# Turning the delta rule's values and outputs, and two attention heads' rows, in 32x32 blocks on VectorE, with the blocks put in their places by the DMA that stores or loads the tile

## The chip, the cores and the metric

The kernel runs on one core of one Trainium2 chip. The metric is the device time of one execution in microseconds (us). Before the change three executions took 1235.09, 1235.05 and 1234.37 us, so the median is 1235.05 us.

## The reference: what is computed

One decoder layer on x of 1024 tokens by 1024 features, all float32. A first RMS norm feeds one input projection `proj = h @ w_in`, whose columns go to two groups that mix the tokens:

- differential attention, 4 heads with two 64-wide softmax maps and 128-wide values: `(softmax(q1 k1^T) - lam * softmax(q2 k2^T)) v`, then an RMS norm per head;
- a gated delta rule, 4 heads, key and value width 128. q, k and v pass a causal convolution of width 4 and SiLU, q and k are normalised, and a state is carried over chunks of tokens:

```
v_new = u - w @ state
o     = (q * exp(g)) @ state + qk @ v_new
state = state * exp(g_last) + k_dec^T @ v_new
```

The output o is normalised per head and multiplied by `silu(z)`.

```
x = x + concat(da_o, dn_o) @ w_out
x = x + square(relu(rms_norm(x) @ w_up)) @ w_down
```

## The kernel before the change, in words

A matmul contracts over the partition axis, so an operand has to lie with the contracted feature on the 128 partitions. Where a tile lies with tokens on the partitions it is turned first. Before the change every such turn is a transpose on TensorE (PE) against an identity matrix: it lands in a PSUM bank, from which VectorE (DVE) or ScalarE (ACT) takes it. The big products keep float32 accuracy by splitting each operand into a rounded part and a rest (`hH`/`hL`, `wH`/`wL`) and doing three fp32r matmuls.

The kernel runs in these stages, with line numbers of the profile:

1. Norm, z and gates (lines 306 to 645).
2. The delta rule's projection, `dn_proj` (666), for k, then q, then v. Each call gives one head h and one half hf of the tokens, 512 tokens, with features on the partitions. For v the loop of lines 851 to 857 turns the four 128x128 tiles on PE (`transposed`, 713, recorded at line 716), scales them by the column `vsc` with one DVE operation (854) and writes them with `park` (701), one DMA of 256 KB, to slot 2 of `park_d` in DRAM. `horner` (797) inverts the chunk matrices for two heads at a time with short dependent matmuls (810, 818), between the v tiles. Its blocks are loaded by 32 small DMAs (804).
3. From line 880 on the order of PE's instructions is written by a planner, `Interleave` (39 to 105). Streams of work yield the time from which they may go on and the PSUM bank they need. The planner keeps a clock of its own with estimated costs, and `flow.hold` says until when a bank is taken. The planner fixes the order for PE alone. The orders on DVE, ACT, GpSimd (POOL) and SyncE (SP) are made by a scheduler when the kernel is built. Every engine then takes its instructions strictly in order. The streams, in order of priority:
   - `scan` (902): the state recurrence over 8 chunks c. `load(c)` (907) brings four 192 KB pieces, one per head, from `park_d` into one of two `pka` buffers (910). Four matmuls (918) feed a DVE operation on slot 2 of `pka` (922), and four more (930), a copy (932), four more (941) and the new state (947) follow.
   - `scan_out` (956): the chunk's output. Matmuls (970, 977), a sum of squares (984), a reciprocal root, four DVE products with the gate (989) and a DMA on POOL's queue (991) that writes the 128x512 tile `oc` to `mixn_d`.
   - `da_turns` (1020): turns the attention's q and k (1028, 1029) in one of the two `px` PSUM banks and stores them from POOL's queue (1034).
   - `mix_loads` (1287) and `mixed` (1298): loads each tile `mt` of `mixn_d` (1295) and each tile of attention rows, and turns all four 128-column blocks on PE (`turn`, 1278, through `to_hT`, 293, transposes at 298) in a `px` bank, then ACT and DVE write `hH` and `hL` (303, 304). A tile's place in `hH` is free only when the last input projection unit is done with that tile.
   - `values` (1222): for each head and block of queries the transposes of the probabilities (1238), the product with the values (1250) in a `px` bank, an ACT copy (1259) and square (1260), a reciprocal root, and a DVE product (1264). Heads 0 and 1 write their rows to `mixa_d` (1266); for heads 2 and 3 the tile `rows_of[tb]` is loaded with the two first heads' rows (1231) and filled up.
   - `scores` (1141), `da_units` (1041, the input projection for the attention, lines 1067 to 1069) and `outproj` (1325, the output projection, lines 1340 to 1342).

   The reciprocal roots (`rstd`, 288) go through POOL's power operation (291): named `rn` for the attention's q and k norm, `of` for the outputs.
4. The MLP, products at lines 1515 to 1517 and 1813 to 1815, which ends the kernel.

`add` registers a stream with its priority, and the planner's loop takes the first stream that may go on:

```python
    flow.add(0, scan(), SCAN_START)
    flow.add(2, values())
    flow.add(3, scores())
    flow.add(1.6, da_turns())
    flow.add(4, da_units())
    flow.add(1.4, mix_loads())
    flow.add(1.5, mixed())
    flow.add(5, outproj())
```

The functions that the diff touches, as they were:

Of the kernel before, what the change touches and what calls it, by code (L numbers as in the profile page):

```python
# [9 lines left out]
F32 = mybir.dt.float32  # L10
# [110 lines left out]
def tile_hymba_layer(  # L121
# [579 lines left out]
    def park(h, hf, slot, src):  # L701
        nc.sync.dma_start(park_d[h, 4 * hf:4 * hf + 4, :, slot, :].rearrange("c p d -> p c d"), v4(src))

    def cols4(t, h, hf):
        return t[:, 8 * h + 4 * hf:8 * h + 4 * hf + 4]

# [142 lines left out]

    heads = [((h, h + 1), hf) for hf in range(2) for h in (0, 2)]  # L850
    for h, hf, v2 in skew(dn_proj(2)):
        ps = transposed(v2)
        vs = ta("kn", 2)
        V.tensor_tensor(v4(vs), v4(ps), bc_col(cols4(vsc, h, hf)), ALU.mult)
        park(h, hf, 2, vs)
        if hf == 0:
            horner(*heads.pop(0))

# [43 lines left out]
    def scan():  # L902
        St = {}
        psA = pA.tile([P, 512], F32, name="ps_A")
        PA = {h: psA[:, h * P:(h + 1) * P] for h in range(HEADS)}

        def load(c):
            pka = sb.tile([P, HEADS, 3, P], F32, tag="pka", name="pka", bufs=2)
            for h in range(HEADS):
                nc.sync.dma_start(pka[:, h], park_d[h, c, :, 0:3, :])  # L910
            return pka

        nxt = load(0)
        for c in range(NT):
            pk, rr_, yy = nxt, {}, {}
            if c > 0:
                for h in range(HEADS):
                    T.matmul(PA[h], pk[:, h, 0, :], St[h], start=True, stop=True)
                for h in range(HEADS):
                    i = cidx(h, c)  # L920
                    rr_[h] = sb.tile([P, P], F32, tag="sr", name="sr", bufs=4)
                    V.scalar_tensor_tensor(rr_[h], PA[h], neg_eg[:, i:i + 1], pk[:, h, 2, :], ALU.mult, ALU.add)
                flow.pe(4 * MM)
                yield flow.chain(*[vec(P, 60)] * 4), None
            else:
                for h in range(HEADS):
                    rr_[h] = pk[:, h, 2, :]
            for h in range(HEADS):
                Wc = W[h, c // 4][:, (c % 4) * P:(c % 4 + 1) * P]
                T.matmul(PA[h], Wc, rr_[h], start=True, stop=True)  # L930
            y4 = sb.tile([P, 512], F32, tag="sy", name="sy", bufs=2)
            S.copy(y4, psA)
            if c + 1 < NT:
                nxt = load(c + 1)
            flow.pe(4 * MM)
            yield flow.chain(act(512)), None
            Sold = dict(St)
            for h in range(HEADS):
                yy[h] = y4[:, h * P:(h + 1) * P]
                if c < NT - 1:  # L940
                    T.matmul(PA[h], pk[:, h, 1, :], yy[h], start=True, stop=True)
            if c < NT - 1:
                for h in range(HEADS):
                    i = cidx(h, c)
                    Sn = sb.tile([P, P], F32, tag=f"S{h}", name=f"S{h}", bufs=2)
                    if c > 0:
                        V.scalar_tensor_tensor(Sn, St[h], elast[:, i:i + 1], PA[h], ALU.mult, ALU.add)
                    else:
                        V.tensor_copy(Sn, PA[h])
                    St[h] = Sn  # L950
                flow.pe(4 * MM)
            flow.add(1, scan_out(c, Sold, yy), 0, "pB")
            if c < NT - 1:
                yield flow.chain(*[vec(P, 60)] * 4), None

    def scan_out(c, Sold, yy):
        pkb = {}
        for h in range(HEADS):
            pkb[h] = sb.tile([P, 2, P], F32, tag="pkb", name="pkb", bufs=5)
            nc.sync.dma_start(pkb[h], park_d[h, c, :, 3:5, :])  # L960
        zgt = sb.tile([P, 512], F32, tag="zgt", name="zgt", bufs=1)
        nc.sync.dma_start(zgt, zg_d[c])
        oc = sb.tile([P, 512], F32, tag="oc", name="oc", bufs=2)
        so = sb.tile([P, 4], F32, tag="so", name="so", bufs=2)
        osq = sb.tile([P, P], F32, tag="osq", name="osq", bufs=1)
        yield flow.now + 2500, "pB"
        if c > 0:
            o1 = pB.tile([P, 512], F32, tag="pB", name="ps_o1")
            for h in range(HEADS):
                T.matmul(o1[:, h * P:(h + 1) * P], pkb[h][:, 0, :], Sold[h], start=True, stop=True)  # L970
            V.tensor_tensor(v4(oc), v4(o1), bc_col(eg[:, c::8]), ALU.mult)
            flow.pe(4 * MM)
            flow.hold("pB", flow.chain(vec(512)))
            yield flow.now, "pB"
        o2 = pB.tile([P, 512], F32, tag="pB", name="ps_o2")
        for h in range(HEADS):
            T.matmul(o2[:, h * P:(h + 1) * P], pkb[h][:, 1, :], yy[h], start=True, stop=True)
        if c > 0:
# [16 lines left out]
        flow.chain(*[act(P, True)] * 4, vec(4), powr(4), vec(4), *[vec(P, 60)] * 4, start=t)  # L995
# [226 lines left out]
    def values():  # L1222
        for _ in order:
# [3 lines left out]
            if h == 2:  # L1227
                while "ax" not in pools or len(rows_of) + len([x for x in loads if not x[3]]) > 1:
                    yield flow.now + 50, None
                rows_of[tb] = pools["ax"].tile([P, 512], F32, tag="mx", name="mx", bufs=2)  # L1230
                nc.sync.dma_start(rows_of[tb][:, 0:256], mixa_d[tb])
            ats = []
            for g in range(0, tb + 1, 4):
                r = yield from flow.bank("px")
# [29 lines left out]
            V.scalar_tensor_tensor(om, om, f, dawb, ALU.mult, ALU.mult)  # L1264
            if h < 2:
                nc.gpsimd.dma_start(mixa_d[tb, :, h * P:(h + 1) * P], om)
            flow.pe((tb + 1) * MM)
            t = flow.chain(act(P))
            flow.hold(r, t)
            t = flow.chain(act(P, True), vec(1), powr(1), vec(1), vec(P, 60), start=t)  # L1270
# [5 lines left out]
    landed, hns = {}, {}  # L1276

    def turn(r, src, t, tb, k0, keep=None):
        to_hT(src, tb, lambda: bank_tile(px, r, "ps_tr"), k0, 4, keep)
# [7 lines left out]
    def mix_loads():  # L1287
        while not (pre and state["scan"]):
            yield flow.now + 200, None
        for i, t in enumerate(tiles):  # L1290
            while i >= 2 + state["mixed"]:
                yield flow.now + 50, None
            mt = pools["a2"].tile([P, 512], F32, tag="mt", name="mt", bufs=2)
            with tc.issue_after(newest["SP"].ins):
                nc.sync.dma_start(mt, mixn_d[t])
            loads.append((mt, flow.now + MIX_T, t, 4))

    def mixed():
        for i in range(2 * NT):

            while not any(x[1] <= flow.now and x[2] in over for x in loads):
                yield flow.now + 50, None
            x = min((x for x in loads if x[2] in over), key=lambda x: x[1])
            r = yield from flow.bank("px")
            loads.remove(x)
            turn(r, *x)
            state["mixed"] += x[3] == 4
        while not state["attn"]:
            yield flow.now + 50, None
        scctx.close()  # L1310
# [607 lines left out]
```

## Time and profile before

| | |
|---|---|
| median of three executions | 1235.05 us |
| the profiled execution | 1234.74 us |
| its span, first to last instruction | 1233.0 us |
| PE busy | 1217.3 us, 99% of the span |
| DVE busy | 824.7 us, 67% |
| ACT busy | 624.2 us, 51% |
| POOL busy | 151.3 us, 12% |
| bytes moved by DMA | 202.12 MB, mean 164 GB/s |
| granted TensorE clock | 1.000 |

The profile shows one execution. It has a page with shares and groups of instructions, and its trace can be asked for the instructions of a line or of a tile, for a stretch of time, for waits, and for the chain of work that ended last. PE's records overlap: a matmul's record lasts from its start to its last result, while the next one starts long before, so the busy share says that PE is never without a record, not how fast it goes. The step from one start to the next is the cost of a matmul.

### The profile page before, as it was taken

The numbers are of one execution on the slowest core, as the hardware profiler recorded it, in microseconds if no ns is written. First come the engines' busy times: TensorE is split into PE (matmuls) and PEld (weight loads), VectorE is DVE, ScalarE is ACT, GpSimd is POOL, SyncE is SP. The second block draws the span as 40 slices with busy tenths as digits, with TensorE's granted clock in tenths as the row PEclk, the third lists the DMA queues.
The fourth block names the chain that finished last, engine by engine and source line by source line (L and its number), as shares of the span: only waits on it lengthen the run. The fifth ranks groups of instructions, "written<-read, shape, count | busy, mean of one in ns | idle before, by whom it ended". The sixth has DMA issues, their size and how long they took to land.

```text
span 1233.0 us, 18819 instructions
## 1 busy us (share of the span) xinstructions
PE 1217.3 (99%) x6823; PEld 1054.3 (86%) x6823; DVE 824.7 (67%) x1524; ACT 624.2 (51%) x1249; POOL 151.3 (12%) x215
## 2 busy tenths in 40 slices
PE   9999999999999999999999999999999999999998
PEld 8978888898999998888888888888888888888886
DVE  6868796556647657777799544565569755777543
ACT  6588553344346555566666544444564333333330
POOL 2411110043434421001200000000000000000000
PEclk9999999999999999999999999999999999999999
DMA  9344653278748756323437434444479645423301
GB/s 350 98 115 122 163 162 104 63 234 240 231 148 252 232 162 159 85 77 108 157 117 255 172 122 151 171 170 153 155 241 382 234 179 184 163 103 103 137 35 69
DMA packets 143301, 202.12 MB, mean 164 GB/s; under 512 B 20920, under 2 KB 98280, under 8 KB 143208
## 3 DMA queue, kind: packets, MB, share of 16 engines
q1 hardware_dynamic: 138584, 187.28, 46.9%
q0 software_dynamic: 4480, 13.64, 2.9%
q8 instruction: 54, 0.88, 0.3%
q14 instruction: 39, 0.32, 0.1%
q10 hardware_dynamic: 144, 0.00, 0.0%
HBM read 135.86 MB, written 65.01 MB: 163 GB/s over the span
## 4 chain that ended last, share of the span: by engine, by line
PE 88%; DVE 4%; DMA 3%; ACT 2%; issue 2%; POOL 1%; SPq 1%; POOLq 0%; DVEq 0%; ACTq 0%
PE X L1517 4%; PE X L1515 4%; PE X L1516 4%; PE X L1814 4%; PE X L1815 4%; PE X L1813 4%; PE ps_dn L265 3%; PE ps_dn L267 3%; PE ps_dn L266 3%; PE ps_qk L1067 3%; PE ps_qk L1068 3%; PE ps_qk L1069 3%; PE ps_o L1250 2%; PE Y L1515 2%; PE Y L1517 2%; PE Y L1516 2%
## 5 line engine op out<-in xcount | busy, mean ns | idle before, releaser
L1433 ACT CAST hH<-ur 128x1024 fp32r<-128x1024 f32 x56 | 58.9, 1051 | 173.4 <-PE Y L1814 89.8
L1434 DVE TENSOR_TENSOR hL<-ur,hH 128x1024 fp32r<-128x1024 f32 x56 | 68.3, 1223 | 79.4 <-ACT hH L1433 79.4
L1067 PE MATMUL ps_qk<-wH,hH 128*128 128x256 f32 x384 | 114.3, 298 | 0.0
L1069 PE MATMUL ps_qk<-wH,hL 128*128 128x256 f32 x384 | 108.7, 283 | 0.0
L1068 PE MATMUL ps_qk<-wL,hH 128*128 128x256 f32 x384 | 108.4, 282 | 0.0
L1434 DVE TENSOR_TENSOR op<-raw,op 128x1024 fp32r<-128x1024 f32 x48 | 58.7, 1223 | 74.2 <-PE X L1516 41.1
L1813 PE MATMUL X<-hH 128*128 128x512 f32 x224 | 87.1, 389 | 0.0
L1814 PE MATMUL X<-hL,hH 128*128 128x512 f32 x224 | 87.1, 389 | 0.0
L1815 PE MATMUL X<-hH,hL 128*128 128x512 f32 x224 | 87.1, 389 | 0.0
L265 PE MATMUL ps_dn<-hH,wH 128*128 128x512 f32 x192 | 76.3, 397 | 0.2 <-ACT cp L678 0.2
L267 PE MATMUL ps_dn<-hH,wL 128*128 128x512 f32 x192 | 75.8, 396 | 0.0
L266 PE MATMUL ps_dn<-hL,wH 128*128 128x512 f32 x192 | 75.8, 395 | 0.0
L1068 PEld LDWEIGHTS ps_qk<-wL,hH 128*128 128x128 f32 x384 | 73.4, 191 | 0.2
L1067 PEld LDWEIGHTS ps_qk<-wH,hH 128*128 128x128 f32 x384 | 73.3, 191 | 0.2
L1069 PEld LDWEIGHTS ps_qk<-wH,hL 128*128 128x128 f32 x384 | 73.1, 190 | 0.0
L1434 DVE TENSOR_TENSOR hL<-dw,hH 128x1024 fp32r<-128x1024 f32 x56 | 68.2, 1218 | 0.9 <-ACT hH L1433 0.9
L1433 ACT CAST op<-raw 128x1024 fp32r<-128x1024 f32 x48 | 50.4, 1052 | 35.7 <-PE Y L1517 19.9
L1433 ACT CAST hH<-dw 128x1024 fp32r<-128x1024 f32 x56 | 58.7, 1048 | 10.7 <-DMA dw<-in_w_down_dram 5.0
L1205 ACT ACTIVATE pexp<-pexp,mx 128x128 f32<-128x128 f32 (+7 forms) x64 | 49.7, 777 | 25.1 <-DVE mx L1204 24.5
L682 DVE SCALAR_TENSOR_TENSOR cy<-cp,pv,cy 128x512 f32<-128x512 f32 x72 | 53.7, 747 | 8.1 <-ACT cy L680 7.3
L1340 PE MATMUL ps_op<-wH,hH 128*128 128x512 f32 x128 | 53.0, 414 | 0.0
L1515 PE MATMUL Y<-hH,op 128*128 128x512 f32 x128 | 49.9, 390 | 0.4 <-DVE ua L1555 0.4
(370 smaller groups left out, 3429.1 us busy)
## 6 DMA issues: line engine op xcount, KB each, us to landing
ur<-ud SPq DMA_DIRECT2D x28, 1024.0 KB, 5.0
raw<-in_w_up_dram SPq DMA_DIRECT2D x32, 512.0 KB, 3.9
dw<-in_w_down_dram SPq DMA_DIRECT2D x32, 512.0 KB, 6.8
wraw<-in_w_units_dram SPq DMA_DIRECT2D x48, 256.0 KB, 3.7
qk_d<-qa POOLq DMA_DIRECT2D x32, 256.0 KB, 4.3
ud<-ua SPq DMA_DIRECT2D x16, 512.0 KB, 4.2
ud<-s SPq DMA_DIRECT2D x16, 512.0 KB, 2.7
pka<-park_d SPq DMA_DIRECT2D x32, 192.0 KB, 4.8
```

What stands on the lines that cost most here:

```text
L265: T.matmul(ps, lh(k), rh(k), start=(k == 0), stop=False)
L266: T.matmul(ps, lh(k), rl(k), start=False, stop=False)
L267: T.matmul(ps, ll(k), rh(k), start=False, stop=(k == n - 1))
L1067: T.matmul(ps[:, :256], hH[:, k, sl], wh[:, k, :], start=(k == 0), stop=False)
L1068: T.matmul(ps[:, :256], hH[:, k, sl], wl[:, k, :], start=False, stop=False)
L1069: T.matmul(ps[:, :256], hL[:, k, sl], wh[:, k, :], start=False, stop=(k == KB - 1))
L1433: S.copy(dst[0], src)
L1434: V.tensor_tensor(dst[1], src, dst[0].bitcast(F32), ALU.subtract)
L1515: T.matmul(ps, op[0][:, k, cs], h[0][:, k, :], start=start and k == 0, stop=False, skip_group_check=True)
L1813: T.matmul(bank[t], v[0][:, j, sl], v[2][:, j], start=s0, stop=False, skip_group_check=True)
L1814: T.matmul(bank[t], v[0][:, j, sl], v[3][:, j], start=False, stop=False, skip_group_check=True)
L1815: T.matmul(bank[t], v[1][:, j, sl], v[2][:, j], start=False, stop=s1, skip_group_check=True)
```

## The change

VectorE has an operation that transposes each 32x32 block of a tile in its own place. To make a 128x128 transpose of it, block (a, b) has still to go to place (b, a). The change does the first half on DVE and lets a DMA do the second.

- v tiles: the four PE transposes and the DVE scaling go. DVE block-transposes the 128x512 tile, and four DMAs (`put_blocks`) write it to `park_d` in pieces of 32 elements. The scaling by `vsc` moves into the scan: `scale(c, pk)` on POOL, one product on the 128x4x128 slot 2 of each `pka` buffer, after its load.
- scan outputs: the four products write into `zgt` instead of `oc`, DVE block-transposes `zgt` into `oc`, and the store to `mixn_d` is unchanged. `mix_loads` reads each tile with four DMAs (`get_blocks`). The tile then lies with features on the partitions, and `mixed` only writes `hH` and `hL` from it (`settle`), with no PE transpose and no `px` bank.
- heads 0 and 1: the DVE product writes to PSUM, into the third quarter of the bank that held the result, a DVE block transpose brings it to `om`, and the bank is planned as held until then. The rows are read with `get_blocks`, and `turn_last` turns only the two blocks of heads 2 and 3 on PE.

```diff
+    def put_blocks(dst, src):
+        for a in range(4):
+            s = slice(32 * a, 32 * a + 32)
+            nc.sync.dma_start(dst[:, s].rearrange("(b s) r -> s b r", s=32),
+                              src[s].rearrange("s (b r) -> s b r", r=32))
+
+    def get_blocks(dst, src):
+        k = dst.shape[1] // P
+        src = src.rearrange("(a s) (k b r) -> b s k a r", s=32, k=k, r=32)
+        for b in range(4):
+            nc.sync.dma_start(dst[32 * b:32 * b + 32].rearrange("s (k a r) -> s k a r", k=k, r=32), src[b])
...
     for h, hf, v2 in skew(dn_proj(2)):
-        ps = transposed(v2)
         vs = ta("kn", 2)
-        V.tensor_tensor(v4(vs), v4(ps), bc_col(cols4(vsc, h, hf)), ALU.mult)
-        park(h, hf, 2, vs)
+        V.transpose(vs, v2)
+        put_blocks(park_d[h, 4 * hf:4 * hf + 4, :, 2, :].rearrange("c p d -> (c p) d"), vs)
...
+        def scale(c, pk):
+            G.tensor_tensor(pk[:, :, 2, :], pk[:, :, 2, :], bc_col(vsc[:, c::8]), ALU.mult)
+
         nxt = load(0)
+        scale(0, nxt)
...
             flow.add(1, scan_out(c, Sold, yy), 0, "pB")
+            if c + 1 < NT:
+                scale(c + 1, nxt)
...
-            V.scalar_tensor_tensor(oc[:, h * P:(h + 1) * P], oc[:, h * P:(h + 1) * P], f[:, h:h + 1],
-                                   zgt[:, h * P:(h + 1) * P], ALU.mult, ALU.mult)
+            hs = slice(h * P, (h + 1) * P)
+            V.scalar_tensor_tensor(zgt[:, hs], oc[:, hs], f[:, h:h + 1], zgt[:, hs], ALU.mult, ALU.mult)
+        V.transpose(oc, zgt)
         nc.gpsimd.dma_start(mixn_d[c], oc)
...
-                nc.sync.dma_start(rows_of[tb][:, 0:256], mixa_d[tb])
+                get_blocks(rows_of[tb][:, 0:256], mixa_d[tb])
...
+            if h < 2:
+                V.scalar_tensor_tensor(po[:, 2 * P:3 * P], om, f, dawb, ALU.mult, ALU.mult)
+                V.transpose(om, po[:, 2 * P:3 * P])
+                nc.gpsimd.dma_start(mixa_d[tb, :, h * P:(h + 1) * P], om)
+                flow.hold(r, flow.chain(act(P, True), vec(1), powr(1), vec(1), vec(P, 60), vec(P, 60), start=t))
+                continue
...
+    def settle(src, tb, ks, t=None):
+        sl = slice(tb * P, (tb + 1) * P)
+        sv = src.rearrange("p (k t) -> p k t", t=P)
+        S.copy(hH[:, ks, sl], sv)
+        V.tensor_tensor(hL[:, ks, sl], sv, hH[:, ks, sl].bitcast(F32), ALU.subtract)
...
+    def turn_last(r, src, t, tb):
+        settle(src[:, 0:256], tb, slice(0, 2))
+        ps = bank_tile(px, r, "ps_tr")
+        for j in (2, 3):
+            T.transpose(ps[:, j * P:(j + 1) * P], src[:, j * P:(j + 1) * P], ident)
...
-                nc.sync.dma_start(mt, mixn_d[t])
+                get_blocks(mt, mixn_d[t])
...
+            if x[3] == 4:
+                loads.remove(x)
+                landed[x[2], 4] = settle(x[0], x[2], slice(4, 8))
+                state["mixed"] += 1
+                continue
             r = yield from flow.bank("px")
             loads.remove(x)
-            turn(r, *x)
-            state["mixed"] += x[3] == 4
+            turn_last(r, *x[:3])
```

More of the change, by code (lines that the diff above doesn't have):

```diff
@@ L994, in scan_out @@
         flow.hold("pB", t)
-        flow.chain(*[act(P, True)] * 4, vec(4), powr(4), vec(4), *[vec(P, 60)] * 4, start=t)
+        flow.chain(*[act(P, True)] * 4, vec(4), powr(4), vec(4), *[vec(P, 60)] * 4, vec(512, 100), start=t)
         if c == NT - 1:
@@ L1263, in values @@
             V.tensor_tensor(f, f, ri[:, 0:1], ALU.mult)
-            V.scalar_tensor_tensor(om, om, f, dawb, ALU.mult, ALU.mult)
-            if h < 2:
-                nc.gpsimd.dma_start(mixa_d[tb, :, h * P:(h + 1) * P], om)
             flow.pe((tb + 1) * MM)
             t = flow.chain(act(P))
+            if h < 2:
[4 more added lines that the diff above has]
+                continue
+            V.scalar_tensor_tensor(om, om, f, dawb, ALU.mult, ALU.mult)
+            t = flow.chain(act(P, True), start=t)
             flow.hold(r, t)
-            t = flow.chain(act(P, True), vec(1), powr(1), vec(1), vec(P, 60), start=t)
+            t = flow.chain(vec(1), powr(1), vec(1), vec(P, 60), start=t)
             if h == 3:
@@ L1276, in tile_hymba_layer @@
     landed, hns = {}, {}
+    def settle(src, tb, ks, t=None):
[3 more added lines that the diff above has]
+        V.tensor_tensor(hL[:, ks, sl], sv, hH[:, ks, sl].bitcast(F32), ALU.subtract)
+        n = P * (ks.stop - ks.start)
+        return flow.chain(act(n), vec(n), start=t)
+    def turn_last(r, src, t, tb):
[3 more added lines that the diff above has]
+            T.transpose(ps[:, j * P:(j + 1) * P], src[:, j * P:(j + 1) * P], ident)
+        flow.pe(2 * TR)
+        t = settle(ps[:, 256:512], tb, slice(2, 4))
+        flow.hold(r, t)
+        landed[tb, 0] = t
     def turn(r, src, t, tb, k0, keep=None):
```

## The prediction, made before the changed kernel ran

> **What bounds the kernel now.** I read the page's shares first, then its slices, then the shares of the chain that ended last.
>
> ```profile
> span 1233.0 us, 18819 instructions
> PE 1217.3 (99%) x6823; PEld 1054.3 (86%) x6823; DVE 824.7 (67%) x1524; ACT 624.2 (51%) x1249; POOL 151.3 (12%) x215
> PE   9999999999999999999999999999999999999998
> PE 88%; DVE 4%; DMA 3%; ACT 2%; issue 2%; POOL 1%; SPq 1%; POOLq 0%; DVEq 0%; ACTq 0%
> ```
>
> PE is busy in every slice and carries 88% of the chain. Next, the view by stage: columns are the stretch and its length, busy us of PE, of its weight loads, of DVE, ACT and POOL, then clock, DMA share and GB/s.
>
> ```profile
> 185.00:256.00 71.00, 70.40 (x538) 61.98 (x537) 42.83 (x85) 24.75 (x59) 3.82 (x5) 1.00 0.33 95
> 256.00:350.00 94.00, 90.69 (x774) 89.81 (x773) 58.14 (x177) 41.63 (x126) 37.55 (x48) 1.00 0.74 231
> 350.00:460.00 110.00, 108.35 (x881) 105.97 (x881) 68.06 (x207) 65.80 (x182) 46.13 (x67) 1.00 0.70 206
> 460.00:585.00 125.00, 123.89 (x737) 108.28 (x736) 92.06 (x248) 77.25 (x203) 15.15 (x28) 1.00 0.38 107
> 640.00:1233.00 593.00, 588.14 (x2593) 486.49 (x2592) 374.70 (x344) 258.59 (x261) 0.00 (x0) 1.00 0.47 167
> ```
>
> The v tiles fall in 185 to 256, the scan in 256 to 350, the turned scan outputs from 430 to 460, the attention rows up to 585. In these four PE is without a record for 0.6 to 3.3 us, most in the scan (94.00 - 90.69), and its clock is 1.00. DVE is idle for a third of the time, POOL for most. So PE work taken away is time saved, unless the replacement makes PE wait. The MLP after 640 is not touched.
>
> **What goes: 80 transposes.** Records overlap, so a transpose costs its step, not its record. The chain of waits shows steps in a row of transposes of the probabilities, each count one more than the last; the timeline of PE shows one turned tile among projection matmuls.
>
> ```profile
> 468.14 0.55 PE ps_at L1238 x5
> 474.87 0.66 PE ps_at L1238 x6
> 482.87 0.77 PE ps_at L1238 x7
> ```
>
> ```profile
> 446.91 0.60 PE L298 MATMUL ps_tr<-ident,mt 128*128 128x128 f32 x4
> 447.26 0.36 PE L1067 MATMUL ps_qk<-wH,hH 128*128 128x256 f32 x1
> 447.46 0.28 PE L1068 MATMUL ps_qk<-wL,hH 128*128 128x256 f32 x1
> 447.58 0.28 PE L1069 MATMUL ps_qk<-wH,hL 128*128 128x256 f32 x1
> ```
>
> One more transpose costs 0.11 us. Without the tile, 1067 would start at 446.91 and 1068 at 447.03 (the usual step is 0.12, 447.46 to 447.58); it started at 447.46, so four cost 0.43, again 0.11 each. The counts:
>
> ```profile
> L716 PE MATMUL ps_t<-ident,k x64: 270/272/329, 82.7 to 232.9; 128*128 128x128 f32 x64
> L716 PE MATMUL ps_t<-ident,cth x32: 270/272/329, 141.9 to 240.9; 128*128 128x128 f32 x32
> L298 PE MATMUL ps_tr<-ident,mt x32: 270/272/273, 431.3 to 459.1; 128*128 128x128 f32 x32
> L298 PE MATMUL ps_tr<-ident,mx x32: 270/272/273, 517.4 to 582.5; 128*128 128x128 f32 x32
> ```
>
> The 96 at 716 turn k, q and v, eight tiles of four each, so 32 are v's. All 32 of `mt` go, and of `mx` the two blocks of heads 0 and 1 in each of eight tiles, 16. So 32 + 32 + 16 = 80, and 80 x 0.11 = **8.8 us**. This is an upper bound where PE stays fed.
>
> The Trainium skill, in "TensorE: Matmul & The Clock Gate", Part 4, prices a 128x128 PE transpose at about 275 ns in a kernel. The records here last as long (270/272/329), but PE goes on after 0.11. By the page's figure 80 would be 22.0 us, my estimate; I take the step.
>
> **v tiles, DVE and stores.** DVE loses a scaling and gains a block transpose of the same shape:
>
> ```profile
> L854 DVE TENSOR_TENSOR kn<-ps_t,vsc x8: 650/683/692, 190.1 to 242.0; 128x512 f32<-128x512 f32 x8
> L806 DVE STREAM_TRANSPOSE W<-gb x8: 690/702/712, 196.8 to 241.4; 128x512 f32<-128x512 f32 x8
> L702 SPq DMA_DIRECT2D park_d<-kn x16: 370/378/642, 90.2 to 242.7; - x16
> gb<-fsg_d SPq DMA_DIRECT2D x32, 16.0 KB, 1.9
> ```
>
> That is +0.02 each, beside 28 us of idle DVE in that stage: nothing. The store becomes four DMAs in 128-byte pieces, 24 more issues of some 0.4 us on SP, no work of PE's. They stand ahead of the inverse's block loads and of the first `pka` loads. No row shows a 64 KB store in such pieces; the nearest is the inverse's `gb`, 16 KB in 128-byte pieces, 1.9 us to landing. What counts is the last v tile, before the scan's first product:
>
> ```profile
> 249.42 3.66 SPq L910 DMA_DIRECT2D pka<-park_d  x8
> 256.56 1.06 PE L930 MATMUL ps_A<-pka,W 128*128 128x128 f32 x8
> ```
>
> It is stored at about 242.7, its loads are issued at 249.42, and 256.56 is the first use: some 7 us of cover on one side. Meanwhile PE has projection units, so a late chunk only shifts fill work. Lower end 0; upper end 2.1, a product on POOL (1.29, below) and two issues (0.4 each) with no fill left. I take **+0.5**, nearer to the covered row.
>
> The Trainium skill, "DMA: Bandwidth & Descriptors", calls pieces below 512 bytes inefficient, which speaks against all three placements. The 128-byte transfer above still lands in under 2 us, and the sum hides it.
>
> **The scaling on POOL.** Eight products of 128x512 in the scan, each waiting for four `pka` loads, with whatever follows on POOL queued behind. No row shows this product; the nearest are these, and the landing is the tile's own:
>
> ```profile
> L1370 POOL TENSOR_TENSOR hn<-hn,w2b x4: 1284/1290/1707, 586.0 to 606.8; 128x512 f32<-128x512 f32 x4
> L291 POOL TENSOR_TENSOR rn<-rnt,neghalf x32: 1006/1032/1345, 246.0 to 428.1; 128x4 f32<-128x4 f32 x32
> DMA to landing us min/median/max: 2.4/4.8/6.4
> ```
>
> POOL has 94.00 - 37.55 = 56.4 us free in this stage, so 8 x 1.29 = 10.3 us fits as throughput. The operand is loaded one chunk ahead, so the product itself is not late. The harm is the order: a `rn` or a store `qk_d` behind it waits up to the landing. A late `rn` delays this chain:
>
> ```profile
> 255.97 1.02 POOL L291 TENSOR_TENSOR rn<-rnt,neghalf 128x4 f32<-128x4 f32 x1 [0.23 <-DVE rnt L290]
> 257.03 0.43 DVE L1092 TENSOR_TENSOR qn<-qn,rn 128x256 f32<-128x256 f32 x1 [1.21 <-POOL rn L291]
> 259.77 0.27 PE L1028 MATMUL ps_qkt<-ident,qn 128*128 128x128 f32 x1
> PE ps_qkt L1028 <- DVE qn L1092: 1.3, 2, 1.0
> ```
>
> Here `qn` ended at 257.46 and PE turned it at 259.77, 2.3 us of cover; but PE already waited for it twice, 1.3 us together. The planner knows nothing of POOL's queue, so a product held for longer than the cover reaches PE whole. Lower end 0.3 (one `rn` held as in its own spread, 1345 - 1032; less than nothing is excluded, since POOL loses no work), upper end 8 x 1.29 = 10.3 plus one shortest landing, 2.4: 13. I take **+2.0**, nearer to the rows with cover: two of the seven products in mid-scan cost about 1 us each, as the longest wait above did.
>
> The Trainium skill, "SBUF — State Buffer", Who interferes with whom, says that a DVE instruction with two SBUF inputs and a GpSimd instruction reading SBUF block each other fully. The spread of 1284 to 1707 fits a partial hold. As an estimate by that page, eight products would hold DVE for 10.3 us, beside 36 us of idle DVE in this stage.
>
> **Scan outputs.** A DVE transpose of 0.70 is added after four products, 8 x 0.70 = 5.6 us on an engine with a third of its time free. `zgt` has one buffer, so its reload on SP waits 0.7 us longer, with the `pka` loads behind it; this is inside the wait priced above. The loads of `mt` become four:
>
> ```profile
> mt<-mixn_d SPq DMA_DIRECT2D x8, 256.0 KB, 3.4
> L1295 SPq DMA_DIRECT2D mt<-mixn_d x8: 319/350/585, 417.7 to 450.9; - x8
> ```
>
> They begin at 417.7, the first turn was at 431.3, the tiles are used from about 460 on. 13 us of cover for three more issues and a longer landing: 0. If that cover went, one landing, 3.4 us, would show once.
>
> **Heads 0 and 1.** The product is written to the bank that held the result, and block-transposed, so the bank is held past ACT's copy to the end of the transpose:
>
> ```profile
> 369.77 0.26 ACT L1259 COPY om<-ps_o 128x128 f32<-128x128 f32 x1
> 371.61 0.19 ACT L1260 ACTIVATION_READ_ACCUMULATOR ps_o<-om,ri 128x1 f32 x1
> 375.27 0.35 DVE L1264 SCALAR_TENSOR_TENSOR om<-om,of,dawb 128x128 f32<-128x128 f32 x1
> L1231 SPq DMA_DIRECT2D mx<-mixa_d x8: 326/332/407, 500.2 to 572.6; - x8
> ```
>
> The bank is released at about 371.8 before, at 375.27 + 0.35 + 0.2 to 0.35, say 375.9, after: 4.1 us longer in this row, 16 times. There are two such banks for turns, probabilities and values; the tiles' turns leave them (eight of `mt`). The planner holds the bank in its own clock, so it puts other units between; what it underestimates stalls PE. Lower end -1.6, the whole time without PE records in 350 to 460, since the eight turns leave the banks; upper end 16 x 0.5 = 8, half a microsecond of each hold. I take **+1.0**, two of the 16 at 0.5, nearer to the lower end, since fill work stands beside it until 585. The `mx` loads are issued 10 to 17 us before their turns (500.2 against 517.4, 572.6 against 582.5), so three more issues cost 0; without that cover one landing of about 2 us.
>
> **Sum** against the profiled execution, 1234.74 (span 1233.0 and 1.74 around it), which is 0.31 below the median of 1235.05: 1234.74 - 8.8 + 0.5 + 2.0 + 1.0 = 1229.4, against the median 1229.7. Its own range, by half to 1.8 times the additions of 3.5, is 1228.0 to 1232.5.
>
> **Rivals.**
> - *All hidden.* 1234.74 - 8.8 = 1225.9, 1226.3 by the median. For: idle time of DVE and POOL. Against: POOL's order.
> - *The bank gives it back.* Its upper end: -8.8 + 8 + 0.5 + 2.0 = +1.7, 1236.4, or 1236.8. For: a hold over four us longer than the row of before. Against: the planner knows it.
> - *POOL's queue becomes the scan's clock (slower).* Each of seven mid-scan products holds `rn` and `qk_d` until its loads have landed (4.8 median) and run (1.29), 6.1 us, less the 2.3 us of cover, 3.8; in the built order about half of them have a `rn` close behind: 3.8 x 3.5 = 13. -8.8 + 13 + 1.5 = +5.7, 1240.4, or 1240.8. It decides from (8.8 + 0.2 x 12.35 - 1.5)/7, about 1.4 us of stall per product. For: three `pka` loads stand behind `zgt`'s reload on SP. Against: in many places more fill work than that stands behind the turn.
> - *Each transpose was worth its whole record*, 0.272: -21.8 + 3.5, 1216.4, or 1216.7. The steps speak against it. The skill's price above leads here too.
> - *The pieces make transfers slow enough to starve PE* is contained in the first two bounds; loads have 7 and 13 us.
>
> **Chances.** Forecast 0.49, all hidden 0.10, bank 0.19, POOL 0.21, whole record 0.01. What a measurement of this kernel can tell from no change is about 0.2%, 2.5 us: 1232.6 to 1237.5. Faster 0.49 + 0.10 + 0.01 = 0.60, same 0.19, slower 0.21. The range 1224.6 to 1241.0 takes in each end of an unknown taken by itself, and leaves out the last rival and some of POOL's and the bank's spread to either side, under 0.2.
>
> **What would show it.** Step: PE's instructions fall by 80, while the starts beside 446 come 0.43 earlier for each tile. POOL: in 256 to 350 its `scale` products show what ended their wait, and the waits of 1028 stay near 1.3 us in the forecast, 10 or more in the last but one rival. Bank: waits of 1238 and 1250 for DVE in 350 to 585 under 2 us in the forecast, 8 or more in that rival. Start: the first `ps_A` near 256.56 less 3.5 (32 x 0.11) plus 0.5. The prediction would be wrong if PE's time without work in 256 to 350 grew by over 5 us, or the chain ran through POOL or SP there.

## The result: slower, and where the time went

The changed kernel took 1245.38 us (median of four executions, 1242.19 to 1248.24) where before took 1234.71: a ratio of 1.0086, 95% interval 1.0061 to 1.0111. That is outside the range given, on the side of the rival that had 0.21. The profiled execution, the fastest of the four, took 1242.19; its span is 1240.4, 7.4 more than before's 1233.0.

The page of the changed kernel, the lines that answer to those of before:

```profile
span 1240.4 us, 18827 instructions
PE 1215.4 (98%) x6743; PEld 1048.1 (85%) x6743; DVE 834.6 (67%) x1556; ACT 624.7 (50%) x1257; POOL 160.4 (13%) x223
PE   9999999998999999999899999999999999999998
POOL 2411110044434431002200000000000000000000
PE 85%; DMA 6%; DVE 2%; ACT 2%; SPq 2%; issue 1%; POOL 1%; DVEq 0%; POOLq 0%; ACTq 0%
```

PE has 6743 matmuls, exactly 80 fewer. Two slices are no longer full, one in the scan and one at the end of the attention, and the chain spends 6% on DMA where it spent 3%. The stages, with the columns as before (length; busy PE, PEld, DVE, ACT, POOL; clock; DMA):

```profile
185.00:256.00 71.00, 70.53 (x530) 61.81 (x529) 43.62 (x83) 26.97 (x63) 5.78 (x6) 1.00 0.46 102
256.00:350.00 94.00, 85.67 (x711) 84.08 (x710) 58.41 (x174) 37.20 (x110) 42.34 (x53) 0.98 0.68 216
350.00:460.00 110.00, 107.94 (x875) 105.44 (x875) 73.14 (x223) 66.19 (x189) 47.08 (x68) 1.00 0.74 209
460.00:585.00 125.00, 123.29 (x719) 106.39 (x718) 94.14 (x256) 76.80 (x206) 15.87 (x27) 1.00 0.39 107
585.00:640.00 55.00, 50.62 (x247) 40.70 (x246) 41.60 (x84) 36.22 (x85) 10.07 (x13) 0.94 0.42 143
```

And the last stage in before, which the prediction had not looked at:

```profile
585.00:640.00 55.00, 54.26 (x271) 45.01 (x269) 44.56 (x77) 34.66 (x74) 9.79 (x12) 1.00 0.41 137
```

I call **lost PE time** of a stretch its length less PE's busy time, plus (1 - clock) times its length. In the scan (256 to 350) it was 3.3 and is 94.00 - 85.67 + 0.02 x 94 = 10.2. In 585 to 640 it was 0.7 and is 4.4 + 0.06 x 55 = 7.7. The two stretches between lost 1.0 more together. So 6.9 + 7.0 + 1.0 - 8.8 for the transposes = +6.1 of the 7.4; the clock's two digits leave about one us open.

**The first loss: POOL's queue in the scan.** The scalings' line, and from the waits in 256 to 350 (total us, times, longest) POOL's for their loads and PE's:

```profile
L927 POOL TENSOR_TENSOR pka<-pka,vsc x8: 1039/1048/1052, 252.1 to 333.7; 128x512 f32<-128x512 f32 x8
```

```profile
POOL pka L927 <- DMA pka<-park_d: 14.8, 5, 5.5
```

```profile
PE ps_qkt L1048 <- DVE qn L1112: 5.9, 5, 1.8
PE ps_o L989 <- DMA pkb<-park_d: 1.8, 1, 1.8
```

The product takes 1.05 us, less than assumed, but POOL stands idle before it for 14.8 us, waiting for `pka`. `rn` is behind it, and PE waits five times for what `rn` scales (twice in before, 1.3 us). Of the 6.9 us about 4.6 are these waits, 0.6 is a longer wait for a `pkb` load (1.2 in before) and 1.9 the clock. In this execution the clock fell behind the stop for `pkb`; that POOL's product makes `pkb` late is not shown.

**The second: the end of the attention.** The last product with the values starts at 578.0 in before and at 588.9 after. The rows give that, and what is left of the output projection from there on (one of its three lines); the last is PE's longest wait in 460 to 640:

```profile
L1250 PE MATMUL ps_o<-vt,at x288: 270/275/275, 369.1 to 578.0; 128*128 128x128 f32 x144
L1340 PE MATMUL ps_op<-wH,hH x46: 389/389/474, 578.0 to 613.8; 128*128 128x512 f32 x46
```

```profile
L1270 PE MATMUL ps_o<-vt,at x288: 270/275/377, 371.3 to 588.9; 128*128 128x128 f32 x144
L1387 PE MATMUL ps_op<-wH,hH x33: 389/393/481, 589.0 to 618.7; 128*128 128x512 f32 x33
```

```profile
PE ps_tr L1493 <- DVE nrt L290: 3.1, 1, 3.1
```

Of the output projection's matmuls 3 x 46 were left to set beside the last norms in before, 3 x 33 after. PE ran out of them and stood still for a row norm.

**And the clock.** Two gaps lower the granted clock. Windows of a few us around them, and around one that doesn't:

```profile
280.00:285.00 5.00, 3.24 (x28) 3.04 (x28) 3.40 (x12) 2.39 (x9) 2.73 (x3) 1.00 0.86 259
285.00:290.00 5.00, 4.22 (x36) 4.02 (x35) 2.34 (x9) 0.74 (x2) 3.19 (x4) 1.00 0.51 187
298.00:301.00 3.00, 1.17 (x9) 0.85 (x7) 1.12 (x4) 0.00 (x0) 1.77 (x2) 1.00 0.96 252
301.00:306.00 5.00, 5.00 (x30) 5.00 (x30) 3.85 (x11) 1.26 (x3) 0.77 (x1) 0.66 0.70 219
614.00:620.00 6.00, 2.86 (x15) 1.89 (x14) 4.75 (x10) 4.60 (x10) 0.55 (x1) 0.94 0.76 274
620.00:626.00 6.00, 5.18 (x17) 4.00 (x16) 5.08 (x10) 4.28 (x9) 1.08 (x1) 0.50 0.50 175
```

After 1.8 us without work at 298 the clock is 0.66 over the next five us; after 3.1 us at 615 it is 0.50 for six. After 5.00 - 3.24 = 1.8 us at 280 it stays at 1.00. The four executions had mean clocks of 0.996, 0.993, 0.995 and 0.996 for 1242.2, 1248.2, 1245.8 and 1245.0 us: 0.003 of clock is 3.7 of the 6.0 us between the first two. What spreads them beyond that is not shown.

### The profile page after: what moved, and what is told of

It reads as the page before. It is cut to its first block, busy times and chain, and to the rows that moved or that the text cites. A ratio compares the mean times of both kernels' runs of the same rounds, so it can differ in the third digit from the quotient of the medians.

```text
span 1240.4 us, 18827 instructions
## 1 busy us (share of the span) xinstructions
PE 1215.4 (98%) x6743; PEld 1048.1 (85%) x6743; DVE 834.6 (67%) x1556; ACT 624.7 (50%) x1257; POOL 160.4 (13%) x223
## 4 chain that ended last, share of the span: by engine, by line
PE 85%; DMA 6%; DVE 2%; ACT 2%; SPq 2%; issue 1%; POOL 1%; DVEq 0%; POOLq 0%; ACTq 0%
PE X L1562 5%; PE X L1564 5%; PE X L1563 5%; PE X L1861 4%; PE X L1860 4%; PE X L1862 4%; PE ps_dn L265 3%; PE ps_dn L267 3%; PE ps_dn L266 3%; PE Y L1564 2%; PE Y L1562 2%; PE Y L1563 2%; PE ps_qk L1087 2%; PE ps_qk L1088 2%; PE ps_qk L1089 2%; PE ps_o L1270 2%
## 5 line engine op out<-in xcount | busy, mean ns | idle before, releaser
L1480 ACT CAST hH<-dw 128x1024 fp32r<-128x1024 f32 x56 | 58.7, 1048 | 10.5 <-DMA dw<-in_w_down_dram 4.8
L1389 PE MATMUL ps_op<-wH,hL 128*128 128x512 f32 x128 | 50.6, 395 | 0.0
```

The costliest lines, as they stand in the source:

```text
L1480: S.copy(dst[0], src)
```

## The experiments

Sixteen kernels ran, each beside runs of before on the same chip; the ratio is to those. Lost PE time in us, worked out from each profile's windows as above. Some expectations give the loss as "time over the steps", another count of it that runs higher: 18.3 in e1's scan, where the table has 15.2.

| kernel | us | ratio, 95% interval | 256-350 | 350-460 | 460-585 | 585-640 |
|---|---|---|---|---|---|---|
| before | 1235 | | 3.3 | 1.7 | 1.1 | 0.7 |
| after | 1245.4 | 1.0086 (1.0061, 1.0111) | 10.2 | 2.1 | 1.7 | 7.7 |
| e1 v alone | 1242.8 | 1.0054 (1.0037, 1.0071) | 15.2 | 2.3 | 1.1 | 0.7 |
| e2 scan outputs alone | 1241.0 | 1.0041 (1.0027, 1.0054) | 3.0 | 5.4 | 3.0 | 1.6 |
| e3 rows alone | 1247.0 | 1.0087 (1.0071, 1.0103) | 3.1 | 5.3 | 1.1 | 9.2 |
| e4 all, no POOL scaling | 1239.2 | 1.0029 (1.0019, 1.0038) | 3.3 | 3.4 | 2.4 | 7.3 |
| e5 v, no POOL scaling | 1233.7 | 0.9986 (0.9976, 0.9996) | 6.6 | 1.8 | 1.5 | 0.8 |
| e6 rows, in place | 1240.9 | 1.0045 (1.0029, 1.0061) | 3.2 | 8.1 | 1.6 | 0.8 |
| e7 outputs, four stores | 1242.5 | 1.0055 (1.0040, 1.0069) | 9.7 | 7.0 | 1.3 | 1.6 |
| e8 v, scaling later | 1236.9 | 1.0008 (0.9998, 1.0018) | 6.0 | 2.0 | 1.1 | 0.8 |
| e9 outputs, old order | 1238.2 | 1.0024 (1.0012, 1.0036) | 3.0 | 7.1 | 3.6 | 0.8 |
| e10 rows in place, old order | 1245.0 | 1.0076 (1.0060, 1.0093) | 3.3 | 1.9 | 11.5 | 0.2 |
| e11 all, old order | 1249.0 | 1.0112 (1.0094, 1.0130) | 5.8 | 6.0 | 14.4 | 1.3 |
| e12 rows by bank, old order | 1267.3 | 1.0255 (1.0239, 1.0271) | 3.4 | 23.1 | 5.2 | 6.9 |
| e13 before, four loads | 1247.7 | 1.0094 (1.0067, 1.0121) | 3.5 | 3.7 | 10.5 | 1.9 |
| e14 all, loads on POOL | 1239.1 | 1.0025 (1.0013, 1.0037) | 4.3 | 3.8 | 6.0 | 1.6 |
| e15 old order, on POOL | 1241.8 | 1.0047 (1.0030, 1.0064) | 3.7 | 11.2 | 2.2 | 1.2 |
| e15 old order, on ACT | 1240.9 | 1.0039 (1.0024, 1.0054) | 3.8 | 9.3 | 3.5 | 1.1 |

### The three parts, each alone, and the whole without POOL's scaling

e1, e2 and e3 each make one part of the change's diff in the kernel before. e4 makes all three, and takes the scaling out of the scan:

```diff
         for h in hs:
+            V.tensor_tensor(v4(z[h]), v4(z[h]), bc_col(cols4(vsc, h, hf)), ALU.mult)
             W[h, hf] = z[h]
...
+    V.reciprocal(ssk, vsc)
+    V.tensor_tensor(neg_eg, neg_eg, ssk, ALU.mult)
...
-            if c + 1 < NT:
-                scale(c + 1, nxt)
```

> Only the v part: block transposes, four-piece stores, POOL's eight scalings in the scan; scan outputs and attention rows as before. PE's planned order is that of before without 32 transposes. Queue theory (the scalings hold rn and qk_d behind their loads on POOL, PE runs dry in the scan): -3.5 + 6.5 of added gaps in 256 to 350 + about 1.5 of lower clock after a gap of 2 us there, 1238 to 1240, with waits of line 1028's turns for qn of 5 us or more. Tail theory (the loss arises at the end of the attention, where the longer held bank pushes work back): no tail gap here, 1231 to 1233, waits for qn under 2 us.

> Only the scan outputs are turned in blocks and read back with four loads; v and the attention rows as before. Both the queue and the tail theory: nothing of theirs is in it, -3.5, 1231 to 1232. A third theory (the added DVE transpose and the reload of zgt behind it stretch the scan, or 128-byte pieces are slow): 1236 or more, with longer waits of the scan for zgt's or pka's loads.

> Only heads 0 and 1 are turned in blocks, with the product and the transpose through the held bank; v and the scan outputs as before. Tail theory: -1.8 for 16 transposes, but the attention ends over 8 us later on PE's list than before, the last norm has no output projection left beside it, one PE gap of 3 us or more near 610 and a lower clock behind it: 1238 to 1242. Queue theory: 1233 to 1234, no gap over 1.5 us near 610.

> The whole change, but POOL's scaling in the scan is gone: vsc is multiplied into the rows of W (8 DVE products of 128x512 before the scan) and divided out of neg_eg once, which gives the same output. Queue theory: the gaps and the clock dip in 256 to 350 go, 8 us less than the changed kernel's 1245: 1236 to 1238. Tail theory: only the tail counts, 1243 to 1245, with the gap of 3.3 us near 615 as it was.

All three parts lose by themselves, and at different places, so neither theory is enough. e1 loses 11.9 us more than before in the scan: the queue theory, larger than expected. POOL in e1 around its longest wait, and PE's wait that follows:

```profile
317.04 1.04 POOL L927 TENSOR_TENSOR pka<-pka,vsc 128x512 f32<-128x512 f32 x1 [4.30 <-DMA pka<-park_d]
318.03 0.58 POOL L1010 DMA_DIRECT2D mixn_d<-oc  x1
318.63 1.03 POOL L291 TENSOR_TENSOR rn<-rnt,neghalf 128x4 f32<-128x4 f32 x1
```

```profile
PE ps_qkt L1047 <- DVE qn L1111: 9.4, 6, 4.4
```

POOL idles 4.30 us for the loads, `rn` runs after the product and a store, and PE waits 4.4 us at once; the clock is 0.50 behind it. e3 has the tail theory's loss: 9.2 at the end, for 1.8 of gain. e2 was expected at 1231 by both theories and came at 1241, so a third cause was needed; its PE waited for the scores' q:

```profile
PE ps_sc L1208 <- DMA qa<-qk_d: 2.6, 2, 1.9
```

e4 shows both at once: the scan is back at 3.3 and the tail stays at 7.3. Taking POOL's product out of the change brings the ratio from 1.0086 to 1.0029, about 7 us.

### The v part: the product or its wait?

e5 is the v part with e4's folding. e8 keeps POOL's products, calls each of them from the second on at the start of its own chunk instead of one chunk ahead, and makes it depend on a later result, so that the scheduler sets it later on POOL. The added lines:

```diff
+                col = sb.tile([P, 4], F32, tag="vcol", name="vcol", bufs=2)
+                V.scalar_tensor_tensor(col, St[3][:, 0:4], 0.0, vsc[:, c::8], ALU.mult, ALU.add)
```

> Only the v part, and the scaling folded into W and neg_eg before the scan instead of POOL's eight products. PE's planned order is the one of the v part alone. Queue theory: the time over the steps in 256 to 350 falls from 18.3 us (v part alone) back to about 6, no clock dip, 32 x 0.11 = 3.5 us gained: 1231 to 1233 where before is 1235. If the four-piece stores or the 128-byte pieces cost the scan something: 1236 or more, with a late first ps_A.

> Only the v part with POOL's scaling, but from the second chunk on its column passes through a small DVE operation that reads the chunk's new state, so the scheduler sets the product behind one or two more of rn and qk_d on POOL, when its loads have landed. Queue theory (the wait for the loads at the head of POOL's queue is the cost, not 1.05 us of work): POOL's idle time for pka's loads falls from over 20 us to under 6, the time over the steps in 256 to 350 from 18.3 to 7 to 10, 1233 to 1237. If the product's own time or its SBUF traffic is the cost: 1241 to 1243 as before.

The line of the product in e8 and what POOL waited for before it:

```profile
L931 POOL TENSOR_TENSOR pka<-pka,vcol x7: 1030/1052/1055, 262.7 to 336.5; 128x512 f32<-128x512 f32 x7
...
  DMA pka<-park_d: 9.0, 1
```

The one wait left is the first product's. With the same products of 1.05 us the scan's lost time falls from 15.2 to 6.0, the kernel from 1242.8 to 1236.9: most of the cost is the wait at the head of the queue, not the work. Not all of it: on the same chip e5 is 3.3 us faster than e8, and whether the first product's wait, the products' own time or the small DVE operations make that up was not separated. Without the product (e5) the kernel is faster than before by 0.14% (interval 0.04% to 0.24%), the best of all that ran, and faster than the change. Of the 3.5 us about 2 are measured; in the profiled execution one wait of 2.9 us for a `pkb` load and a clock dip behind it cost 3.3 in the scan.

### The attention rows: the bank and the planner's order

e6 transposes `om` in its own place in SBUF, so that the bank is free after the square. e10 does the same with three `om` buffers, and the planner books what it booked before, so that PE's order is that of before less the transposes. e12 has the change's way through the bank in that same order.

```diff
             if h < 2:
-                V.scalar_tensor_tensor(po[:, 2 * P:3 * P], om, f, dawb, ALU.mult, ALU.mult)
-                V.transpose(om, po[:, 2 * P:3 * P])
+                V.scalar_tensor_tensor(om, om, f, dawb, ALU.mult, ALU.mult)
+                V.transpose(om, om)
```

> Only the attention rows' part, but the product goes to om in SBUF and DVE transposes om in its own place, so the PSUM bank is free after ACT's square as before. Bank theory: the attention's end on PE's list comes back, no gap of 2 us at the end, no clock dip, 1.8 us gained: 1233 to 1236. If not the bank but the four loads of each rows tile on SP are the cost: waits of the scores for qa and qb, 1240 or more.

> Only the attention rows' part, om transposed in its own place in SBUF with three om buffers instead of two, and the planner books what it booked before, so PE's order is that of before without 16 transposes. Order theory: 1.8 us gained, 1233 to 1235, no PE gap over 1.3 us in 350 to 460. If the DVE transposes or the rows' four loads cost of themselves: 1237 or more.

> Only the attention rows' part with the product and the transpose through the PSUM bank as in the change, but the planner books what it booked before, so PE's order is that of before and the longer hold of the bank is met as it comes. Bank theory (the real hold of 4 us more starves PE): waits for line 1264's bank by turns and values of 8 us or more, 1240 to 1250. Order theory (the hold itself is mostly covered, what the planner makes of it costs): 1234 to 1237.

The tail of e6 is 0.8 again: the booked hold of the bank is what spent the output projection early. What is left of it after the last product with the values goes with the loss in 585 to 640: 24 of each line in e3 with 9.2 us, 33 in the changed kernel and e4 with 7.7 and 7.3, 37 in e6 and 46 in before with 0.8 and 0.7. (e12 doesn't fit in this stretch, as its attention itself runs to 609.) But e6 loses 6.4 more than before in 350 to 460. There PE waited 3.6 us for a bank, since ACT could not copy out of it in time:

```profile
385.66 0.27 ACT L1273 COPY om<-ps_o 128x128 f32<-128x128 f32 x1 [2.70 <-DMA mixa_d<-om]
```

The older of the two `om` buffers was still being stored. In e12 PE meets the hold unplanned; its stage, and its waits for the bank over the whole run (11.2 of the 12.7 us in this stage):

```profile
350.00:460.00 110.00, 95.73 (x721) 93.11 (x721) 62.17 (x185) 55.87 (x154) 40.02 (x56) 0.92 0.60 180
```

```profile
PE ps_qkt L1042 <- DVE om L1283: 9.2, 3, 5.0
PE ps_at L1252 <- DVE om L1283: 3.5, 3, 2.0
```

So the bank theory holds: met as it comes, the hold costs e12 21 us in this stage, with 8.8 of them (0.08 x 110) by the clock, and the planner turns that into some 7 us at the end. e10 was to gain 1.8 and lost 10 us in 460 to 585. The profile puts most of its waits there to DVE or to nothing that it shows; the longest ends at 576.6, 2.4 us after the issue of a load of `qa` that stood behind 2.6 us of row loads on SP. That led to the loads.

### The loads: four issues for one

e7 places the blocks of the scan outputs by four stores from POOL's queue and loads the tile at once; e9 has the four loads of the change and the planner's bookings of before; e13 is the kernel before with nothing but the loads changed, so it leaves the blocks of these tiles exchanged and does not compute the reference's output. The four loads make 64 where before has 16 (the expectations' 56 is a miscount):

```diff
-                nc.sync.dma_start(mt, mixn_d[t])
+                get_blocks(mt, mixn_d[t])
...
-                nc.sync.dma_start(rows_of[tb][:, 0:256], mixa_d[tb])
+                get_blocks(rows_of[tb][:, 0:256], mixa_d[tb])
```

> Only the scan outputs' part, but the blocks are placed by four stores from POOL's queue and the tile is read back with one load from SP. The planned order is that of the part alone (the planner counts no issues). SP-queue theory (32 loads of 0.6 to 0.8 us hold the loads of q for the scores): the gap of 2 us at 458 and its clock dip go, the time over the steps in 350 to 585 falls by 4 to 6, 1232 to 1236. Rival (the planned order without the px turns is worse in itself): 1239 to 1241 as with four loads. A cost may appear on POOL in the scan: 24 more issues of 0.6 with rn behind them, in 256 to 350.

> Only the scan outputs' part, with four loads as in the change, but the planner books what it booked before (bank, four transposes, no added DVE time), so PE's order is word for word that of before without the 32 transposes. Order theory (the loss of 9 us in the part alone comes from the order that the planner now makes): 3.5 us gained, 1231 to 1233, time over the steps in 350 to 585 about 8 us as before. SP-queue theory (issues of the four loads hold the loads of q): waits of the scores for qa and qb of 2 us or more stay, 1237 to 1241.

> The kernel before, with only the loads of mt and of the attention rows changed to four each in 128-byte pieces (56 more issues less the 8 + 8 of before, 48). Nothing is transposed on DVE, so the blocks of these tiles reach the output exchanged but not turned; all PE transposes stay and PE's order is that of before. SP-queue theory: the scores wait for qa and qb as in the parts alone, 5 to 14 us over the steps more in 350 to 585, 1240 to 1248. If the DVE transposes or the settling are the cost: 1235 to 1237.

e13 loses 12 us, without a transpose or a bank changed. SP's queue in before at 566, then in e13 at 575 (start, us in issuing); then e13's longest wait of PE, its stage, and the landing of its row tiles:

```profile
566.15 0.33 SPq L1231 DMA_DIRECT2D mx<-mixa_d  x1
566.54 0.45 SPq L1134 DMA_DIRECT2D qb<-qk_d  x1
```

```profile
575.45 2.56 SPq L716 DMA_DIRECT2D mx<-mixa_d  x4
578.06 0.61 SPq L1148 DMA_DIRECT2D qb<-qk_d  x1
```

```profile
PE ps_sc L1208 <- DMA qb<-qk_d: 3.2, 3, 2.6
```

```profile
460.00:585.00 125.00, 118.23 (x695) 103.72 (x694) 86.72 (x231) 72.44 (x187) 14.24 (x25) 0.97 0.40 99
```

```profile
DMA to landing us min/median/max: 2.1/2.2/3.6
```

The pieces land in 2.2 us, as the whole tile did. What costs is SP: one issue took 0.33 us, four take 2.56, and the load of `qb`, for which the scores and PE wait, stands behind them; PE's wait of 2.6 us ends at 580.4, when that `qb` has landed. Whether an issue is long for its 128-byte pieces or for another trait of these loads was not separated. e9 and e7 are in line without being as clean. e9 keeps its waits for q, but its longest wait, 3.0 us at 434, is for a bank. e7 frees SP and its 460 to 585 is 1.3, but its stores on POOL lose 6.4 in the scan, and 350 to 460 stays at 7.0 for reasons that I did not separate.

### All parts together, with the loads on other queues

e11 has all three parts with the scaling folded, `om` in place with three buffers and the planner's old bookings. e15 is e11 with the four loads issued from POOL's, then from ACT's queue; e14 has them on POOL with the bookings of the change, except that the bank is booked as free after the square. The edit for POOL:

```diff
-            nc.sync.dma_start(dst[32 * b:32 * b + 32].rearrange("s (k a r) -> s k a r", k=k, r=32), src[b])
+            nc.gpsimd.dma_start(dst[32 * b:32 * b + 32].rearrange("s (k a r) -> s k a r", k=k, r=32), src[b])
```

> All three parts: scaling folded into W, om in its own place with three buffers, planner's bookings as before, so from the scan on PE has the order of before without 48 transposes. Order theory with the queue theory: the three gains add up, the v part's 1.5 to 2, 3.5 and 1.8: 1227 to 1230. SP-queue theory: the 56 more loads on SP take back 4 or more, 1232 to 1238.

> All three parts as in e11 (scaling folded into W, om in its own place with three buffers, the planner's bookings of before), but the four loads of mt and of the rows are issued from POOL's queue instead of SP's. SP-queue theory: the waits of the scores for q go, the time over the steps in 460 to 585 falls from 16.4 to 3 to 6, 1228 to 1236; on POOL the loads wait for buffers with reciprocal roots behind them, which may give some back in 350 to 460. If SP's queue isn't it: 1245 to 1250 as e11.

> As e15 on POOL, but the four loads are issued from ACT's queue. SP-queue theory: waits of the scores for q go, but ACT gets 56 issues of about 0.6 us, 34 us, between the copies and exponentials on which PE waits: 1232 to 1245. If SP's queue isn't it: 1245 to 1250 as e11.

> All three parts with the planner's bookings of the change (the bank of heads 0 and 1 is free after the square, tiles of scan outputs take no bank), scaling folded into W, om in its own place with three buffers, the four loads on POOL's queue. SP-queue theory: better than the same on SP, 1228 to 1236, and the gap at the end stays under 1.3 us. If the order that the planner makes of it costs of itself: a gap of 2 us or more in 350 to 460, 1237 or more.

e11 is the change with its first two causes removed, and slower still: 14.4 lost in 460 to 585, the four loads on SP. The same on POOL:

```profile
350.00:460.00 110.00, 101.02 (x804) 98.50 (x803) 66.91 (x202) 60.81 (x167) 63.19 (x90) 0.98 0.71 195
460.00:585.00 125.00, 122.79 (x731) 107.10 (x730) 96.49 (x273) 79.59 (x215) 40.35 (x67) 1.00 0.40 106
```

460 to 585 falls from 14.4 to 2.2, so SP's queue is settled as the cause there. But 350 to 460 rises from 6.0 to 11.2. The reciprocal roots share POOL's queue with the loads:

```profile
356.10 5.85 POOL L716 DMA_DIRECT2D mt<-mixn_d  x8 [1.71 <-PE ps_qk L1086]
361.31 1.70 POOL L291 TENSOR_TENSOR rn<-rnt,neghalf 128x4 f32<-128x4 f32 x1
```

Behind these eight issues `rn` ends at 363.0, and PE waits 2.8 us for what it scales. Another 2.2 are the clock (0.02 x 110); the rest was not traced. On ACT the stage loses 9.3, and in e14 the loss moves to 460 to 585, both for reasons that I did not separate. On none of the three queues did the 64 issues leave the kernel as fast as before.

## Why the prediction was wrong

- **"So 32 + 32 + 16 = 80, and 80 x 0.11 = 8.8 us"**: the count is right, and the step for v's 32. 80 matmuls fewer; the first `ps_A` starts earlier by 3.4 where 32 x 0.11 = 3.5 less 0.5 was expected to put it at 253.6:

```profile
L947 PEld LDWEIGHTS ps_A<-pka,W x8: 186/192/192, 253.2 to 254.0; 128*128 128x128 f32 x8
```

  So the +0.5 for the v tiles came to nothing. That the other 48 are worth 0.11 each no run shows by itself: the table's four stretches leave 1.3 us of the changed kernel's span open, 2.8 of e4's and 5.1 of e14's.
- **"I take +2.0, nearer to the rows with cover"**: this step failed. The scan lost 6.9 us in the change and 11.9 with the v part alone, and PE's time without work there grew by the 5 us that were to show the prediction wrong (8.3 against 3.3). The mechanism of the third rival was right and its 13 too high for the change; that its 1240.4 came near is luck, as it had nothing for the tail. I took the cover of a single `qn` for that of all, and priced the wait by before's longest, 1.0 us. POOL stood idle for 14.8 us before it, and e8 shows that this wait, more than the product, is the cost.
- **"The planner holds the bank in its own clock, so it puts other units between"**, +1.0: mis-sized, and sought in the wrong stretch. What it put between was the output projection, which was then missing at the end: 7.0 us in 585 to 640, a stage without a term in the sum. The bank's own sign stayed away in the change: the waits of the probabilities' transposes and products for DVE in 350 to 585 are 0.6 us. Met unplanned, the hold costs 21 us with the clock (e12).
- **"13 us of cover for three more issues and a longer landing: 0"**, and "three more issues cost 0" for the rows: wrong as a rule, though nearly right for the change itself (1.0 us in 350 to 585). Why the change, with the same loads on SP, escapes most of it was not tested. The cover was that of the tile; the loads of q behind it on SP have none. Alone, the issues cost 12 us (e13).
- **The clock** had no term. It fell to half after gaps that the sum had at their bare length, and adds some 5 us here (0.02 x 94 + 0.06 x 55).
- **The 128-byte pieces and the DVE work** were right at nothing: the v stores land in 2.0 us, `mt` in 3.0 and the rows in 2.2, and e5, which has the transposes, the pieces and eight more DVE products, gains.
- **The hold of DVE** was an estimate of 10.3 us beside idle time, and came to two holds of about 0.8 us in the changed kernel: on a small `rnt` at 252.2 (0.95 instead of 0.16) and on `wL`, a DVE operation with two inputs in SBUF. Here are the rows of `wL` in 256 to 350, before and after, then the slow one beside POOL's product:

```profile
L225 DVE TENSOR_TENSOR wL<-wraw,wH x10: 682/689/692, 259.7 to 347.0; 128x512 fp32r<-128x512 f32 x10
L225 DVE TENSOR_TENSOR wL<-wraw,wH x10: 681/691/1448, 257.9 to 350.0; 128x512 fp32r<-128x512 f32 x10
276.01 1.04 POOL L927 TENSOR_TENSOR pka<-pka,vsc 128x512 f32<-128x512 f32 x1 [2.06 <-DMA pka<-park_d]
276.15 1.45 DVE L225 TENSOR_TENSOR wL<-wraw,wH 128x512 fp32r<-128x512 f32 x1 [1.19 <-ACT wH L224]
```

`wL` took 0.76 us longer than usual; 0.90 us of the product were left when it started. In e1 a `wL` came first, and the product beside it took 1.38 us instead of 1.05. The DVE operation that takes `oc` from PSUM was not held: 0.69 us at 286.51 beside the product of 286.61, 0.68 in the mean. By the Trainium skill, "SBUF — State Buffer", Who interferes with whom, a DVE instruction with two SBUF inputs contends with a GpSimd one that reads SBUF, over ports that are an exclusive lock; here the trace agrees. It is not what cost the scan: e8 has five holds of DVE of 0.7 to 0.8 us and loses 6.0 there.

## What to carry to other kernels

In these runs, work taken off a saturated engine was gained only where what replaced it kept nothing waiting at a queue's head. Before moving a step to an idle engine or splitting a DMA, list what stands behind each new instruction on that queue, with the wait of its operands, and who waits for that: here the issue and the wait counted more than the duration and the landing. Where a planner fixes the order, look also at the end of its list, where the filler that it spent earlier is missing.

## What the runs showed of the hardware

A stop of PE can cost more than its length. In the changed kernel, e1, e2 and e12, waits of 1.8 to 5.0 us were followed by granted clocks of 0.50 for 3 to 7 us; yet the stop at 280 in the changed kernel left the clock at 1.00. The Trainium skill, "TensorE: Matmul & The Clock Gate", Part 1, tells of a free-running window of about 3.4 us after whose idling the clock is halved. The half rate and the length of the dips agree; that a stop of 1.8 us can be enough, and at other times is not, goes beyond what it says of a whole idle window.

A DMA issue on SP took 0.33 us for the row tile in one piece and 0.61 for each quarter of it in 128-byte pieces (medians, before and e13), while both land in 2.2 us. Issuing, not moving, was the dear part of placing these blocks by DMA.
